# Norm weights as a row spread by TensorE, the first token tile in two column halves, the second tile's squares behind the first's transposes

## The chip, the cores and the metric

The kernel runs on one core of a Trainium2 chip. A core has a matrix engine (TensorE, PE in the profile), a vector engine (VectorE, DVE), a scalar engine (ScalarE, ACT), a general engine (GpSimd, POOL) and a queue engine (SyncE, SP). They run five separate instruction streams, each in its own order, and wait for one another through semaphores. Loads and stores are issued by SP, by POOL or by ACT and are carried out by 16 DMA engines. The metric is the device time of one execution in microseconds, the median of several runs.

## The reference, cut to what matters

```python
def rmsnorm(x, g):
    y = xf * lax.rsqrt(jnp.mean(xf * xf, axis=-1, keepdims=True) + EPS)
    return (y * g).astype(x.dtype)

def reference(x, mem, g_mix_norm, ..., w_in, ...):          # x (1, 1024, 1024), mem (1, 256, 1024)
    h = rmsnorm(x, g_mix_norm[l])
    proj = jnp.einsum('bsd,de->bse', h, w_in[l])            # w_in (1024, 6664)
    ... stick-breaking attention, forgetting attention, memory attention, gates, w_out
    h2 = rmsnorm(x, g_mlp_norm[l])
    u = jax.nn.relu(jnp.einsum('bsd,df->bsf', h2, w_ff_up[l]))
    x = x + jnp.einsum('bsf,fd->bsd', u * u, w_ff_down[l])
```

Only the first line of the block, the norm of x with its weight `g_mix_norm` (1024 numbers, the same for every token), and the first product after it are touched.

## The kernel before, in words

Every product is made from operands split in two parts, a high one (`hi`, `whi`: rounded by an ACT copy) and a low one (`lo`, `wlo`: what is left, by a DVE subtraction), with three matmuls for one: high x high, low x high, high x low. PE therefore has work for nearly the whole time.

The head is the stretch before the first product. The 1024 tokens come in eight tiles of 128 (x0 to x7), each 128 x 1024 floats, 512 KB. For each tile ACT squares it and sums the rows (`norm`, L421) and takes a root (L347); DVE makes the reciprocal root (`rsqrt_quick`, L352 to L361) and scales the tile by it and by the norm weight, in two column halves (L433); PE turns each half by four transposes (`norm_half`, L449); ACT copies the turned half to `hi` (L457) and DVE makes `lo` (L458). The norm weight lies in `gb`, a 128 x 1024 tile, filled by one DMA that repeats the row for all 128 partitions (`fetch_tokens`, L386). The first weight blocks of `w_in`, called w0 and w1 here (rows 0 to 511 and 512 to 1023 of the same 256 columns), are split by `weight` and `split` (L1038, L1039). The first products (L1128, `natural_ops`) are x0 with w0, x0 with w1, x1 with w0 and so on, 12 matmuls each.

While PE has nothing to do at the head, `warm` (L399) gives it dummy transposes of the identity into a bank that nobody reads, two at a time. They have an effect on PE alone.

What sets the order: nothing here is ordered by hand. Each step is a generator that yields operations with an estimated cost, and a planner (`Machine`) runs them against a model clock when the program is built: whenever an engine of the model is free it takes the ready operation with the smallest due time, and the instruction is written into that engine's stream at that moment. `side=True` work (the products, the dummies) is taken only when nothing else is ready. On the chip each engine then runs its stream strictly in order. A dummy that the planner put in front of a product is therefore run before it, whether the product could already start or not. Two more orders matter: SP's own stream (`fetch_tokens`: x0, norm weight, x1, w0, w1, x2 to x7), and a stretch later (at about 47 to 58 us) where the last tokens, two tiles of `mem` and the sums of `sums_T` (L515 to L525) share DVE with the split of two weight blocks of 264 columns.

Of the kernel before, what the change touches and what calls it, by code (L numbers as in the profile page):

```python
# [21 lines left out]
P = 128  # L22
# [21 lines left out]
def tile_hybrid_block(  # L44
# [67 lines left out]
    root_table()  # L112
# [223 lines left out]
    SN, RS, S1 = tiles(E, "sn", 10, 512), tiles(R, "raw", 4, 1024), R.t("s1", [P, 4, 256])  # L336
    XT = tiles(N, "xt", 7, D)
# [8 lines left out]
    def root(z, ss):  # L346
        nc.scalar.activation(z, ss, AF.Sqrt, bias=eps, scale=CUBE ** -2)  # L347
# [24 lines left out]
    def landed(fn, size, *evs):  # L372

        yield from transfer(fn, size, 0.45, 380e3)
        for ev in evs:
            machine.fire(ev)

    def fetch_tokens(keys):
        for key in keys:
            if key[0] == "w":  # L380
                load, (raw, ev) = h_tasks[0].loads[key[1]], first_raws[key[1]]
                spawn(landed(lambda load=load, raw=raw: fetch(raw, load), P * 1024 * 4, ev))
            elif key[0] == "g":
                gb, ev = gains[key[1]]
                g = g_mix if key[1] == "x" else g_memn
                spawn(landed(lambda gb=gb, g=g: nc.sync.dma_start(gb, g.partition_broadcast(P)), P * D * 4, ev))  # L386
            else:
                xt = yield Get(XT)
                src, i = (x, key[1]) if key[0] == "x" else (mem, key[1])
                x_in[key] = xt, spawn(landed(lambda xt=xt, src=src, i=i: nc.sync.dma_start(  # L390
                    xt, src[i * P:(i + 1) * P, :]), P * D * 4))

# [11 lines left out]
    def norm(keys, late, after=None):  # L404
# [6 lines left out]
        for i, key in enumerate(keys):  # L411
            while key not in x_in:
                yield Sleep(0.1)
            xt, ev = x_in[key]
            yield ev
# [9 lines left out]
        r = yield from rsqrt_quick(ss, z, n)  # L425
        for i, key in enumerate(keys):
# [3 lines left out]
            for k4 in range(2):  # L430
# [4 lines left out]
                evs.append(spawn(norm_half(key, xt, k4, last), late))  # L435
            for ev in evs:
# [4 lines left out]
    def norm_half(key, xt, k4, scaled):  # L441
# [15 lines left out]
        yield Op("ACT", act_time(512), lambda: nc.scalar.activation(hi, tr4, AF.Copy))  # L457
        yield Op("DVE", dve_time(512), lambda: nc.vector.tensor_tensor(lo, tr4, f32(hi), ALU.subtract))  # L458
# [21 lines left out]
    def prologue():  # L480
# [3 lines left out]
        spawn(fetch_tokens([("x", 0), ("g", "x"), ("x", 1), ("w", 0), ("w", 1), *xs, ("g", "m"), ("m", 0), ("m", 1)]))  # L484
        spawn(warm(half_made[2, 1]), 100.0)
        evs = [spawn(norm(ks_, 4.0 * i - 8.0, half_made[AFTER[i]] if i in AFTER else None), 4.0 * i - 8.0)
# [549 lines left out]
    def split(hi, lo, raw):  # L1036
        m = int(np.prod(hi.shape[1:]))
        yield Op("ACT", 0.03 + act_time(m), lambda: nc.scalar.activation(hi, raw, AF.Copy))  # L1038
        yield Op("DVE", dve_time(m), lambda: nc.vector.tensor_tensor(lo, raw, f32(hi), ALU.subtract))  # L1039
# [8 lines left out]
    def weight(pair, load, raw):  # L1048
        _, kk, n = load
        if raw is None:  # L1050
# [5 lines left out]
        else:  # L1056
            raw, ev = raw
            yield ev
        yield from split(pair[0][:, :kk * n], pair[1][:, :kk * n], raw[:, :kk * n])
# [1619 lines left out]
```

## Time and profile before

| | |
|---|---|
| median of 3 runs | 1687.49 us (1686.82 to 1692.76) |
| the profiled execution's own time | 1687.17 us |
| its span, first to last instruction | 1685.3 us |
| PE busy | 1673.1 us (99%) |
| DVE busy | 1291.1 us (77%) |
| ACT busy | 848.4 us (50%) |
| first product starts (L1128) | 11.63 us after the span's start |

The profile's times count from the span's start; 1.9 us of the run's time lie outside the span. Rows of the order in time show the start, the duration, the engine, the line, the operation and the tiles that it writes and reads; in brackets stands the idle time ahead and what ended it. PEld rows are weight loads of PE, which run beside its matmuls; SPq rows are the issue of a DMA, not its transfer. A row's duration ends when the last result is written, so that rows which follow closely overlap, and the pace of a stream is read from the starts.

### The profile page before, as it was taken

The page shows a single profiled execution, that of the slowest core. Times are in us where ns is not written, and L with a number is a line of the kernel's source. Part 1 is how long each engine was busy: PE and PEld are TensorE (multiplying, and loading weights), DVE is VectorE, ACT ScalarE, POOL GpSimd, SP SyncE. Part 2 cuts the span into 40 slices and gives each one's busy share as a digit, 9 for nine tenths or more (in the row PEclk, how much of TensorE's full clock was granted, in tenths as well). Part 3 has the DMA queues.
Part 4 walks back from the last instruction along what each step waited for, and adds up shares of the span by engine and source line. Part 5 has one row for each costly group of instructions (what it writes and reads, how often), then busy time and mean ns, then how long its engine had stood idle before and what let it go on. Part 6 is the DMA issues. An engine that isn't in the chain of part 4 may idle for free.

```text
span 1685.3 us, 25009 instructions
## 1 busy us (share of the span) xinstructions
PE 1673.1 (99%) x9118; PEld 1430.1 (85%) x9118; DVE 1291.1 (77%) x2079; ACT 848.4 (50%) x1474; POOL 256.1 (15%) x441
## 2 busy tenths in 40 slices
PE   9999999999999999999999999999999999999999
PEld 9998899998888888888888887778888887888887
DVE  7977778855459888877787898987777776688775
ACT  6455555534358888876762446533333344332331
POOL 0000000000253151254400011022111120000000
PEclk9999999999999999999999999999999999999999
DMA  7545444567384365387757542144444484564532
GB/s 245 158 150 182 148 120 151 146 195 242 128 240 150 113 185 155 116 252 227 222 163 237 181 156 101 57 167 154 148 151 137 150 309 171 199 208 141 196 125 75
DMA packets 141837, 284.32 MB, mean 169 GB/s; under 512 B 16913, under 2 KB 52817, under 8 KB 141714
## 3 DMA queue, kind: packets, MB, share of 16 engines
q1 hardware_dynamic: 110034, 182.56, 32.0%
q0 software_dynamic: 31680, 100.17, 19.8%
q8 instruction: 72, 1.18, 0.3%
q14 instruction: 51, 0.42, 0.1%
HBM read 189.83 MB, written 92.83 MB: 168 GB/s over the span
## 4 chain that ended last, share of the span: by engine, by line
PE 77%; issue 14%; POOL 3%; DVE 3%; DMA 2%; ACT 1%; SPq 0%; POOLq 0%; ACTq 0%; DVEq 0%
PE pp L1416 11%; PE pp L1128 10%; PE sc L1416 7%; PE pp L2616 7%; PE sc L1128 6%; PE tr L901 4%; PE tr L2616 4%; PE sc L2616 4%; POOL s_scr L1956 3%; PE pv L1416 3%; PE pv L2616 2%; PE sc L918 2%; PE pp L918 2%; PE pp L1939 1%; PE pp L2181 1%
## 5 line engine op out<-in xcount | busy, mean ns | idle before, releaser
L1039 DVE TENSOR_TENSOR wlo<-raw,whi 128x1024 fp32r<-128x1024 f32 (+1 forms) x88 | 107.5, 1221 | 80.6 <-ACT whi L1038 80.4
L1038 ACT ACTIVATE whi<-raw 128x1024 fp32r<-128x1024 f32 (+1 forms) x88 | 93.4, 1061 | 80.3 <-PE pp L1416 32.7
L2616 PE MATMUL pp<-h,sop 128*128 128x512 f32 x540 | 128.5, 396 | 0.0
L2616 PEld LDWEIGHTS pp<-h,sop 128*128 128x128 f32 x540 | 101.4, 188 | 24.6 <-DVE sop L1875 0.2
L1939 PE MATMUL pp<-h,oh 128*128 128x512 f32 x384 | 121.1, 396 | 0.7 <-ACT cu L2024 0.6
L908 DVE TENSOR_TENSOR ptl<-tr,pth 128x512 fp32r<-128x512 f32 (+1 forms) x160 | 98.4, 627 | 23.8 <-ACT pth L906 23.4
L906 ACT ACTIVATE pth<-tr 128x512 fp32r<-128x512 f32 (+1 forms) x160 | 86.8, 558 | 32.3 <-PE sc L918 16.8
L1939 PEld LDWEIGHTS pp<-h,oh 128*128 128x128 f32 x384 | 71.9, 188 | 19.0 <-ACT cu L2024 1.4
L2531 ACT ACTIVATE h<-t 128x2048 fp32r<-128x2048 f32 (+1 forms) x17 | 30.8, 1814 | 110.4 <-DVE t L1875 97.6
L1333 POOL DMA_DIRECT2D raw<-w_in x32 | 24.2, 755 | 394.8 <-DVE wlo L1039 394.8
L1939 PE MATMUL pp<-h,ol 128*128 128x512 f32 x192 | 76.0, 396 | 0.0
L827 DVE TENSOR_TENSOR_SCAN e<-r,e 128x384 f32<-128x384 f32 (+3 forms) x64 | 66.3, 1043 | 6.9 <-ACT e L812 6.4
L1932 ACT ACTIVATE oh<-raw 128x512 fp32r<-128x512 f32 x64 | 39.4, 625 | 61.7 <-DVE raw L1875 61.7
L2616 PE MATMUL sc<-h,sop 128*128 128x512 f32 x264 | 63.6, 396 | 0.2 <-DVE sop L1875 0.2
L1875 DVE TENSOR_TENSOR sop<-ur,sop 128x2048 fp32r<-128x2048 f32 (+1 forms) x28 | 61.7, 2208 | 2.2 <-ACT sop L2544 2.2
L2616 PE MATMUL tr<-h,sop 128*128 128x512 f32 x264 | 63.4, 396 | 0.0
L901 PE MATMUL tr<-ident,e 128*128 128x128 f32 x416 | 62.5, 272 | 0.0
L2616 PEld LDWEIGHTS sc<-h,sop 128*128 128x128 f32 x264 | 49.6, 188 | 12.5 <-DVE sop L1875 0.7
L2616 PEld LDWEIGHTS tr<-h,sop 128*128 128x128 f32 x264 | 49.6, 188 | 12.0
L901 PEld LDWEIGHTS tr<-ident,e 128*128 128x128 f32 x416 | 50.7, 140 | 10.3
L1956 POOL DMA_DIRECT2D s_scr<-cu x48 | 26.0, 542 | 197.6 <-DVE cu L1946 189.1
L1933 DVE TENSOR_TENSOR ol<-raw,oh 128x512 fp32r<-128x512 f32 x64 | 43.1, 688 | 16.8 <-ACT oh L1932 16.8
(568 smaller groups left out, 5338.6 us busy)
## 6 DMA issues: line engine op xcount, KB each, us to landing
ur<-s_scr SPq DMA_DIRECT2D x26, 1024.0 KB
raw<-w_in POOLq DMA_DIRECT2D x42, 512.0 KB, 5.1
raw<-w_up SPq DMA_DIRECT2D x60, 256.0 KB
s_scr<-s POOLq DMA_DIRECT2D x60, 256.0 KB, 2.7
g<-w_down SPq DMA_DIRECT2D x14, 1024.0 KB
s_scr<-cu POOLq DMA_DIRECT2D x48, 256.0 KB, 3.0
h<-sbk_scr POOLq DMA_DIRECT2D x64, 128.0 KB, 3.2
o<-gate_scr SPq DMA_DIRECT2D x32, 256.0 KB
```

The lines of the kernel that those rows point to most:

```text
L827: nc.vector.tensor_tensor_scan(out=back, data0=rho[:, :u][:, ::-1], data1=back, initial=0.0 if last else beta[:, c + u:c + u + 1], op0=ALU ...
L901: nc.tensor.transpose(tr[:, jj * 256 + a * P:jj * 256 + (a + 1) * P], es[a][:, j * P:(j + 1) * P], ident)
L906: yield Op("ACT", act_time(512 - lo_c), lambda: nc.scalar.activation(ph[:, lo_c:], tr[:, lo_c:], AF.Copy))
L908: yield Op("DVE", dve_time(512 - lo_c), lambda: nc.vector.tensor_tensor(pl[:, lo_c:], tr[:, lo_c:], f32(ph[:, lo_c:]), ALU.subtract))
L918: nc.tensor.matmul(pv[0][:, c_:256], pair.v[:, j, b, :], p_[:, jj * 256 + c_:(jj + 1) * 256], start=(k == 0 and n_ == 0 and i == 0), stop= ...
L1038: yield Op("ACT", 0.03 + act_time(m), lambda: nc.scalar.activation(hi, raw, AF.Copy))
L1039: yield Op("DVE", dve_time(m), lambda: nc.vector.tensor_tensor(lo, raw, f32(hi), ALU.subtract))
L1128: nc.tensor.matmul(ps, a_, b_, start=(first and i == 0), stop=(last and i == n - 1))
L1416: nc.tensor.matmul(out_, a_, b_, start=(first and n == 0 and j == 0), stop=(last and n == 3 and j == len(todo) - 1), skip_group_check=True)
L1939: nc.tensor.matmul(ps, w[a_][:, k * P:(k + 1) * P], h[b_][k], start=(first and k == 0 and i == 0), stop=(last and k == 3 and i == 2), skip ...
L1956: nc.gpsimd.dma_start(s_scr[r0:r0 + P, :], t)
L2616: nc.tensor.matmul(ps, a_[:, c, qs], b_[:, c, :], start=(kind in ("P1", "P2", "P7") and c == 0 and i == 0), stop=(kind in ("P2", "P4", "P3 ...
```

## The change

- `g_mix` is no longer loaded 128 times over. ACT issues two DMAs of 512 numbers each, first thing in its stream and ahead of the load of its table, into one partition of two `sn` tiles. PE multiplies a row of ones with each of them (`spread_gain`, one matmul each of 128 columns by 512, in float32), which puts the row into all 128 partitions of a PSUM bank. DVE copies the first bank to `gb`, ACT the second.
- x0 is loaded as two DMAs of 512 columns. Its squares are summed in two steps (`first_squares`): the first half's sum becomes the bias of the root and the start of `v`.
- SP's order becomes x0 (two DMAs), w0, x1, w1, x2 and so on.
- x1's squares wait, in the planner, for the second turned half of x0 (`first_turned`); w0's low part waits for x0's scaling (`first_scaled`), w1's split for `first_turned`.
- The planner's rate for transfers is 240e3 instead of 380e3 bytes per us until three tokens' tiles are under way.

```diff
     def root_table():
         nc.scalar.activation(C.t("st", [P, 8])[:, :1], one, AF.Sqrt)
-    root_table()
...
+    gain_rows, ones = [SN.free.popleft() for _ in range(2)], SN.free.popleft()
+    for c, t in enumerate(gain_rows):
+        nc.scalar.dma_start(t[0:1, :], g_mix[:, c * 512:(c + 1) * 512])
+    root_table()
+    nc.vector.memset(ones[0:1, :P], 1.0)
...
-    def rsqrt_quick(ss, z, n):
+    def rsqrt_quick(ss, z, n, v0=-EPS):
...
-        yield Op("DVE", SMALL, lambda: nc.vector.tensor_scalar(v, ss, -1.0, -EPS, ALU.mult, ALU.add))
+        yield Op("DVE", SMALL, lambda: nc.vector.tensor_scalar(v, ss, -1.0, v0, ALU.mult, ALU.add))
...
-        yield from transfer(fn, size, 0.45, 380e3)
+        yield from transfer(fn, size, 0.45, 380e3 if len(x_in) > 2 else 240e3)
...
+                if key == ("x", 0):
+                    evs = [spawn(landed(lambda xt=xt, c=c: nc.sync.dma_start(
+                        xt[:, c * 512:(c + 1) * 512], x[:P, c * 512:(c + 1) * 512]), P * 512 * 4)) for c in range(2)]
+                    first_half.append(evs[0])
+                    x_in[key] = xt, evs[1]
+                    continue
...
+    def spread_gain():
+
+        gb, ev = gains["x"]
+        yield Sleep(2.0)
+        two = yield Get(PP, 2)
+        evs = []
+        for ps, t in zip(two, gain_rows):
+            evs.append((yield Op("PE", 1.7, lambda: nc.tensor.matmul(
+                ps, ones[0:1, :P], t[0:1, :], start=True, stop=True), goes_on=True)))
+        a_, b_ = two
+        yield evs[0]
+        last = yield Op("DVE", dve_time(512), lambda: nc.vector.tensor_copy(gb[:, :512], a_), goes_on=True)
+        yield evs[1]
+        yield Op("ACT", act_time(512), lambda: nc.scalar.activation(gb[:, 512:], b_, AF.Copy))
...
+    def first_squares(xt, ss, z, bias, v0):
+
+        yield first_half[0]
+        yield Op("ACT", 0.85, lambda: nc.scalar.activation(
+            junk[:, :512], xt[:, :512], AF.Square, scale=D ** -0.5, accum_out=v0))
+        yield Op("DVE", 2 * SMALL, lambda: (
+            nc.vector.tensor_scalar(bias, v0, CUBE ** -2, EPS * CUBE ** -2, ALU.mult, ALU.add),
+            nc.vector.tensor_scalar(v0, v0, -1.0, -EPS, ALU.mult, ALU.add)))
+        yield x_in["x", 0][1]
+
+        def rest():
+            nc.scalar.activation(junk[:, 512:], xt[:, 512:], AF.Square, scale=D ** -0.5, accum_out=ss)
+            root(z, ss, bias)
+        yield Op("ACT", 1.1, rest)
...
-        spawn(fetch_tokens([("x", 0), ("g", "x"), ("x", 1), ("w", 0), ("w", 1), *xs, ("g", "m"), ("m", 0), ("m", 1)]))
+        spawn(fetch_tokens([("x", 0), ("w", 0), ("x", 1), ("w", 1), *xs, ("g", "m"), ("m", 0), ("m", 1)]))
...
+        spawn(spread_gain(), -10.0)
+        evs = [spawn(norm(ks_, 4.0 * i - 8.0, first_turned if i == 1 else half_made[AFTER[i]] if i in AFTER else None),
+                     4.0 * i - 8.0)
...
+            if n_ == 1:
+                yield first_turned
+            elif n_ == 0:
+                after = first_scaled
```

What the planner makes of it is seen in the streams. PE's stream before, from its first instruction through the first products; `ident` is the identity, `pv` the bank of the dummies, `tr` the banks of the transposes, xt_150 is x0 and xt_151 is x1, whi_157 and wlo_158 are w0, whi_159 is w1:

```order
L399 MATMUL pv_134<-ident 128x128 x26
L449 MATMUL tr_132<-ident,xt_150 128x128 x4
L449 MATMUL tr_133<-ident,xt_150 128x128 x4
L399 MATMUL pv_134<-ident 128x128 x26
L1128 MATMUL pp_127<-whi_157,hi_120 128x256
...
L399 MATMUL pv_134<-ident 128x128 x2
L1128 MATMUL pp_127<-whi_159,hi_120 128x256
...
L449 MATMUL tr_133<-ident,xt_151 128x128 x4
L399 MATMUL pv_134<-ident 128x128 x10
```

The same place after the change (L445 are the dummies, L501 the transposes, L1192 the products; sn_133, sn_134 the norm weight's rows, sn_135 the ones, xt_153 x0, xt_154 x1, xt_155 x2, whi_160 w0, whi_162 w1):

```order
L445 MATMUL pv_132<-ident 128x128 x2
L412 MATMUL pp_126<-sn_133,sn_135 128x512
L412 MATMUL pp_127<-sn_134,sn_135 128x512
L445 MATMUL pv_132<-ident 128x128 x18
L501 MATMUL tr_130<-ident,xt_153 128x128 x4
L501 MATMUL tr_131<-ident,xt_153 128x128 x4
L445 MATMUL pv_132<-ident 128x128 x14
L1192 MATMUL pp_125<-whi_160,hi_118 128x256
...
L445 MATMUL pv_132<-ident 128x128 x18
L1192 MATMUL pp_125<-whi_162,hi_118 128x256
...
L501 MATMUL tr_131<-ident,xt_154 128x128 x4
L445 MATMUL pv_132<-ident 128x128 x18
L501 MATMUL tr_130<-ident,xt_155 128x128 x4
```

The two spreading products came in after two dummies; up to the first product with w1 and x1 the dummies went from 64 (26, 26, 2, 10) to 70 (2, 18, 14, 18, 18), and those behind the first product from 12 to 36.

ACT's stream before, from its start (xj is a scratch tile, the squares' sums go to `st`):

```order
L111 ACT_TABLE_LOAD
L111 ACTIVATE st_72<-sm 128x1
L421 ACTIVATE xj_167,st_170<-xt_150 128x1024
L347 ACTIVATE st_171<-st_170,sm 128x1
L421 ACTIVATE xj_167,st_172<-xt_151 128x1024
L347 ACTIVATE st_173<-st_172,sm 128x1
L1038 ACTIVATE whi_157<-raw_163 128x1024
L457 ACTIVATE hi_120<-tr_132 128x4x128
```

And after:

```order
L338 DMA sn_133<-g_mix 1x512
L338 DMA sn_134<-g_mix 1x512
L111 ACT_TABLE_LOAD
L111 ACTIVATE st_150<-sm 128x1
L427 ACTIVATE xj_170,st_189<-xt_153 128x512
L435 ACTIVATE xj_170,st_173<-xt_153 128x512
L351 ACTIVATE st_174<-st_173,st_189 128x1
L418 ACTIVATE gb_168<-pp_127 128x512
L1094 ACTIVATE whi_160<-raw_166 128x1024
L509 ACTIVATE hi_118<-tr_130 128x4x128
L509 ACTIVATE hi_118<-tr_131 128x4x128
L471 ACTIVATE xj_170,st_175<-xt_154 128x1024
```

The squares of x1 moved from ahead of w0's high part to behind x0's turned halves, and the copy of the spread weight stands between x0's root and w0.

DVE's stream before, where the last tokens' low part (L458) meets the sums (L515 to L525) and the two blocks of 264 columns (wlo of 1056):

```order
L458 TENSOR_TENSOR lo_121<-tr_133,hi_120 128x4x128
L515 TENSOR_TENSOR sn_143<-hi_120 128x512
...
L525 TENSOR_TENSOR sn_135<-sn_135,lo_121 128x512
L1039 TENSOR_TENSOR h_752<-sn_144,h_751 128x512
L1039 TENSOR_TENSOR h_750<-sn_143,h_749 128x512
L1039 TENSOR_TENSOR wlo_162<-raw_164,whi_161 128x1056
L1039 TENSOR_TENSOR h_754<-sn_135,h_753 128x512
L1039 TENSOR_TENSOR wlo_158<-raw_163,whi_157 128x1056
```

And after:

```order
L512 TENSOR_TENSOR mt_123<-tr_130,mt_122 128x512
L512 TENSOR_TENSOR mt_123<-tr_131,mt_122 128x512
L571 TENSOR_TENSOR sn_134<-hi_118 128x512
...
L581 TENSOR_TENSOR sn_136<-sn_136,lo_119 128x512
L1097 TENSOR_TENSOR h_779<-sn_135,h_778 128x512
L1097 TENSOR_TENSOR wlo_165<-raw_167,whi_164 128x1056
L1097 TENSOR_TENSOR wlo_161<-raw_166,whi_160 128x1056
```

The last tile ahead of the sums is now one of `mem` (mt) and no longer of x, and one split of a sum instead of two stands ahead of the first wlo, none between the two. Behind about 110 us of the program the streams of all five engines are the same as before.

More of the change, by code (lines that the diff above doesn't have):

```diff
@@ L414, in norm @@
             xt, ev = x_in[key]
+            if key == ("x", 0):
+                two = stat(2)
+                yield from first_squares(xt, ss, z, two[:, 0:1], two[:, 1:2])
+                continue
             yield ev
@@ L424, in norm @@
             yield Op("ACT", 1.25 + 0.22 * last, squares)
-        r = yield from rsqrt_quick(ss, z, n)
+        r = yield from rsqrt_quick(ss, z, n, two[:, 1:2] if keys[0] == ("x", 0) else -EPS)
         for i, key in enumerate(keys):
@@ L1034, in __init__, with split @@
             self.done, self.chosen, self.w = Event(), Event(), []
-    def split(hi, lo, raw):
+    def split(hi, lo, raw, after=None):
         m = int(np.prod(hi.shape[1:]))
         yield Op("ACT", 0.03 + act_time(m), lambda: nc.scalar.activation(hi, raw, AF.Copy))
+        if after:
+            yield after
         yield Op("DVE", dve_time(m), lambda: nc.vector.tensor_tensor(lo, raw, f32(hi), ALU.subtract))
@@ L1049, in weight @@
         _, kk, n = load
+        after = None
         if raw is None:
@@ L1056, in weight @@
         else:
+            n_ = next((i for i, r_ in enumerate(first_raws) if r_ is raw), None)
             raw, ev = raw
             yield ev
-        yield from split(pair[0][:, :kk * n], pair[1][:, :kk * n], raw[:, :kk * n])
+            if n_ == 1:
+                yield first_turned
+            elif n_ == 0:
+                after = first_scaled
+        yield from split(pair[0][:, :kk * n], pair[1][:, :kk * n], raw[:, :kk * n], after)
         RAW.put(raw)
```

14 lines of the change are left out of this document (11 added, 3 removed).

## The prediction

> **What bounds the kernel now.** I read the page's busy table first, then PE's waits over the whole span, then PE's time by stretches, then the head row by row.
>
> ```profile
> PE 1673.1 (99%) x9118; PEld 1430.1 (85%) x9118; DVE 1291.1 (77%) x2079; ACT 848.4 (50%) x1474; POOL 256.1 (15%) x441
> ```
>
> PE is busy but for 12.2 us of 1685.3. Its waits, with what ended them (us in total, times, longest):
>
> ```profile
> PE tr L449 <- DVE xt L433: 1.4, 1, 1.4
> PE pv L399 <- POOL ident masks.py:199: 1.4, 1, 1.4
> PE pp L1128 <- DVE wlo L1039: 1.1, 2, 0.9
> PE pp L1128 <- DVE lo L458: 0.2, 1, 0.2
> ```
>
> Those at the head are 1.4 (x0's scaling), 0.2 and, near 57 us, 1.1. PE's time by stretches (us from the start, length, busy, count):
>
> ```profile
> 6.31:7.72 1.41, 0.01 (x2) 1.00 1.00 373
> 7.72:11.60 3.88, 3.87 (x33) 1.00 1.08 388
> 11.60:19.62 8.02, 7.84 (x67) 1.00 1.05 381
> 19.62:49.96 30.34, 30.34 (x266) 1.00 0.44 145
> ```
>
> From 19.62, the first product of w1 with x1, PE has no gap for 30 us. So whatever the change does to the moment at which PE reaches that product shifts all behind it by as much, until the wait near 57 us. The busy share hides one thing: dummies count as busy. Before the first product the chain that ended last runs through a transfer and not through PE (start, length, what):
>
> ```profile
> 2.12 7.17 DMA raw<-w_in
> ...
> 9.32 1.07 ACT whi L1038
> ...
> 10.41 1.01 DVE wlo L1039
> ...
> 11.55 0.69 DVE lo L458
> ...
> 12.29 1.44 PE pp L1128 x10
> 13.73 0.22 PE pv L399 x2
> ```
>
> w0 lands at 9.3 and its split and x0's low part end at 12.25. The change aims at this chain.
>
> **The change, part by part.** The rows needed, PE's first, then ACT, DVE and SP:
>
> ```profile
> 1.36 4.95 PE L399 MATMUL pv<-ident 128*128 128x128 f32 x26 [1.36 <-POOL ident masks.py:199]
> 7.72 1.32 PE L449 MATMUL tr<-ident,xt 128*128 128x128 f32 x8 [1.40 <-DVE xt L433]
> 8.87 3.00 PE L399 MATMUL pv<-ident 128*128 128x128 f32 x26
> 11.63 0.36 PE L1128 MATMUL pp<-whi,hi 128*128 128x256 f32 x1
> 12.29 0.38 PE L1128 MATMUL pp<-whi,lo 128*128 128x256 f32 x1 [0.18 <-DVE lo L458]
> 12.51 0.28 PE L1128 MATMUL pp<-whi,hi 128*128 128x256 f32 x1
> 13.45 0.28 PE L1128 MATMUL pp<-whi,lo 128*128 128x256 f32 x1
> 19.62 0.36 PE L1128 MATMUL pp<-whi,hi 128*128 128x256 f32 x1
> ```
>
> ```profile
> 0.74 1.28 ACT L111 ACT_TABLE_LOAD   x1 [0.74 <-PEq L2668]
> 4.75 1.06 ACT L421 ACTIVATE xj<-xt 128x1024 f32<-128x1024 f32 x1 [2.52 <-DMA xt<-x]
> 5.71 0.19 ACT L421 ACTIVATION_READ_ACCUMULATOR xj<-xt 128x1 f32 x1
> 5.94 0.30 ACT L347 ACTIVATE st<-st,sm 128x1 f32<-128x1 f32 x1
> 7.82 1.06 ACT L421 ACTIVATE xj<-xt 128x1024 f32<-128x1024 f32 x1 [1.58 <-DMA xt<-x]
> 10.28 1.07 ACT L457 ACTIVATE hi<-tr 128x512 fp32r<-128x512 f32 x2
> ```
>
> ```profile
> 6.91 1.41 DVE L433 SCALAR_TENSOR_TENSOR xt<-xt,st,gb 128x512 f32<-128x512 f32 x2
> 10.41 1.23 DVE L1039 TENSOR_TENSOR wlo<-raw,whi 128x1024 fp32r<-128x1024 f32 x1 [0.47 <-ACT whi L1038]
> 11.55 1.28 DVE L458 TENSOR_TENSOR lo<-tr,hi 128x512 fp32r<-128x512 f32 x2
> ```
>
> ```profile
> 0.74 0.39 SPq L390 DMA_DIRECT2D xt<-x  x1
> 1.18 0.42 SPq L386 DMA_DIRECT2D gb<-g_mix  x1
> ```
>
> *Paces.* 26 dummies fill PE's stream from 8.77 (the weight load of the first) to 11.60, 0.109 each; products go at (13.45 - 12.51)/8 = 0.1175. The early dummies take longer, as two windows of PE's dummies show:
>
> ```profile
> 1.30:3.30 2.00, 1.94 (x9) 1.94 (x10) 1.00 0.68 221
> 5.30:6.30 1.00, 1.00 (x9) 0.78 (x7) 1.00 0.99 381
> ```
>
> 9 in 2.0 us, later 9 in 1.0: 0.22 against 0.11. 25 steps from 1.36 to the last start at 5.93 give 17 at 0.22 and 8 at 0.11, so PE went to full speed near 5.2, 3.9 us after its first dummy.
>
> *Transfers.* The broadcast of the norm weight (512 KB) leaves the queue. x0 is there at 4.75 and x1, with that broadcast between, at 7.82: about 1.5 us for 512 KB. So w0 lands at 4.75 + 1.6 = 6.4 instead of 9.3, x1 at 7.9 (unchanged), w1 at 9.4, x2 and all behind it 1.5 us earlier. The extra issue of x0's second half costs SP 0.4 us, hidden behind the transfers that already run.
>
> *Norm weight.* ACT's two DMA issues (0.39 each, as SP's) put its table load from 0.74 to 1.6 and the end of it to 3.1, hidden: ACT is idle until 4.75. When the rows land no row shows. The DMA's rate in slices of 0.3 us gives the bounds:
>
> ```profile
> GB/s 0 0 0 0 0 27 205 150 410 369 314 382 273 232 259 218 314 232 369 423 396 423 335 379 375 389 376 389 358 362 358 379 355 423 437 396 410 396 382 396
> ```
>
> The first bytes move in 1.5 to 1.8, the lower end is 1.8; the upper is 4.75, if the rows arrive with x0. x0's 512 KB have moved by 3.5 and ACT sees them at 4.75, 1.25 later; 1.8 and some 1.0 of such a lag give 2.8, which I take. Then the two float32 products of 512 columns. No row has a float32 product that is no transpose: four dummies at 0.22 hold 512 columns and take 0.9, the lower end; twice that, 1.8, is my upper end for full precision, and I take 1.7, near the upper end, since all other products here run in the split format. They end at T0 = 2.8 + 3.4 = 6.2. DVE's copy (about 0.65, as half of L458's 1.28) is done by 5.2, ACT's (half of L457's, 0.55) by 6.9.
>
> *x0.* Its second half lands with the whole tile's bytes, 4.75. Half the squares are left: 0.55 instead of 1.06, so L433 starts at 6.4 instead of 6.91 and the first transpose may go at 7.2 instead of 7.72. x1's squares, put behind x0's turned halves, cost nothing: PE needs x1 only at about 16.
>
> *PE's stream.* This decides. From T0 to the first product of w1 with x1 stand 18 + 14 + 18 + 18 = 68 dummies, 24 transposes and 36 products. Transposes cost about a dummy: 92 x 0.109 + 36 x 0.1175 = 14.26. The same counting for before, from 12.29 (34 products, 12 dummies, 16 transposes), gives 7.05 where the trace has 7.33, so I add 0.3 for changes between kinds: T0 + 14.56. With T0 = 6.2 that is 20.76; 3 of the first dummies fall before full speed (6.7, that is 3.9 after 2.8), 0.3 more: 21.1. Before it was 19.62. **+1.45.** Nothing else is as late: transposes of x0 at 6.2 + 0.3 + 18 x 0.109 = 8.5 (its scaled half is there at 7.2), first product at 8.5 + 22 x 0.109 = 10.9, a good 0.7 earlier than 11.63, with w0's split done at 9.2 and x0's first low part at about 10.4; on ACT x0's turned halves are copied by 10.1, x1's squares and root done by 11.6 (1.55), w1's high part by 12.7 (1.06), its low part on DVE by 13.9 (1.23), where PE wants it at 10.9 + 1.4 + 18 x 0.109 = 14.3. So the chain through w0 is shortened as meant, and PE then gives the time back on 24 more dummies behind the first product (24 x 0.109 = 2.6).
>
> *Near 57 us.* DVE's rows there:
>
> ```profile
> 49.17 0.68 DVE L515 TENSOR_TENSOR sn<-hi 128x512 f32<-128x512 f32 x1
> 55.31 1.26 DVE L1039 TENSOR_TENSOR wlo<-raw,whi 128x1056 fp32r<-128x1056 f32 x1
> 57.09 1.25 DVE L1039 TENSOR_TENSOR wlo<-raw,whi 128x1056 fp32r<-128x1056 f32 x1
> ```
>
> The 1.1 us are 0.9 for the first wlo and 0.2 for the second. With one split less ahead (0.6), but the last tile turned later (one of `mem`), I leave the 0.9 as it is, between 0 and 1.8; the second wlo now follows the first directly, and its 0.2 goes. Behind that place the streams are the same.
>
> *Sum.* +1.45 - 0.2 = +1.25 on the profiled execution's 1687.17: **1688.4**. The median before, 1687.49, is 0.3 above that execution.
>
> **A rule that would raise it.** The trace has one step of PE to full speed, 3.9 us after the first dummy. The Trainium skill, in TensorE: Matmul & The Clock Gate, Part 1, says that the array runs at half speed until a free-running window of about 3.4 us has been busy, and that the moment varies with where the window falls; 3.9 agrees. By that rule the gap that PE now has between its second dummy and the first row's landing may cost a window: full speed then comes between 6.2 and 9.6.
>
> **The rivals.** *PE's full speed comes late.* If a product with one row of 128, or the gap ahead of it, doesn't count, the 3.9 us start with the dummies at 6.2. All 18 then take 0.22, 18 x 0.109 = 2.0 more instead of 0.3: +1.45 + 1.7 - 0.2 = +2.9, 1690.1. Against it speaks that the early dummies needed no full load either; for it, that no row shows a one-row product. *Not slower:* the float32 products are cheap (0.9 each, T0 = 4.6), and PE waits for x0 again. Its transposes, the 50 dummies behind them and the rest are 74 x 0.109 + 36 x 0.1175 + 0.3 = 12.6, so PE arrives earlier than 19.62 if x0's first transpose starts before 7.0, that is if the second half lands before 4.5. Landing at 4.2 gives 6.7 and -0.3; with the 0.2 that is 1686.7. For it speaks the rate row: x0's bytes have moved by 3.5. Against it, the 4.75 at which ACT saw the same bytes. *The weight comes no sooner than the tokens* (the change doesn't do what it says): rows at 4.75, T0 = 8.15 at full speed in the second half, 22.7, +3.1 - 0.2, 1690.1.
>
> **How the numbers follow.** Forecast (PE runs its stream from the spread on, +0.3 to +2.4 by the bounds of the landing and of the product) 0.60, 1688.4. Late full speed 0.20, cheap spread 0.12, late rows 0.08. The range takes in the first two rivals' times and 0.4 for the runs' spread around their median, and a wait near 57 us half gone below: 1686.3 to 1691.0. All cases lie within 0.5% (8.4 us, about what a measurement of this kernel can tell from no change): 0.97; 0.01 faster; 0.02 slower, for a place downstream that I haven't seen.
>
> **What would show it.** In the profile of the changed kernel: w0's high part should start before 8 us (right: the transfer moved up); the first product before 11.3; PE without a wait from the spread to 21 us, with 18 dummies between the products of w0 and of w1; the first product of w1 with x1 near 21.1; the two L412 matmuls about 1.7 apart. A gap of PE ahead of x0's transposes would show the cheap spread; dummies at 0.22 behind the spread, the late full speed. Wrong I am if PE waits behind the first product, so that the dummies cost nothing, or if the stall near 57 us changes by more than 0.5.

## The result, and the profile after

The changed kernel takes 1692.40 us (median of 12 runs, 1691.02 to 1696.03); the kernel before, run beside it, 1688.98 (median of 12, 1686.51 to 1692.76). The ratio is 1.002, with a 95% interval of 1.0012 to 1.0028: slower by 2.0 to 4.7 us. That is clear of noise, and still within the bound of 0.5% under which the prediction counts two times as the same. The profiled execution took 1695.19 us with a span of 1693.4, 8.1 more than the span before.

PE in order of time from the first instruction (start, duration, what, idle time ahead in brackets); L445 are the dummies, L412 the spreading products, L501 the transposes, L1192 the products:

```profile
1.36 0.69 PE L445 MATMUL pv<-ident 128*128 128x128 f32 x2 [1.36 <-POOL ident masks.py:199]
2.40 3.75 PE L412 MATMUL pp<-sn,sn 1*128 1x512 f32 x4 [0.35 <-DMA sn<-g_mix]
6.08 4.10 PE L445 MATMUL pv<-ident 128*128 128x128 f32 x18
9.97 1.64 PE L501 MATMUL tr<-ident,xt 128*128 128x128 f32 x8
11.44 1.69 PE L445 MATMUL pv<-ident 128*128 128x128 f32 x14
12.89 0.36 PE L1192 MATMUL pp<-whi,hi 128*128 128x256 f32 x1
...
14.39 2.12 PE L445 MATMUL pv<-ident 128*128 128x128 f32 x18
...
18.64 2.13 PE L445 MATMUL pv<-ident 128*128 128x128 f32 x18
...
22.89 0.28 PE L1192 MATMUL pp<-whi,hi 128*128 128x256 f32 x1
```

The last row is the first product of w1 with x1: 22.89 where it was 19.62, 3.27 later. Three groups of 18 dummies stand in this piece. The later two take 2.12 and 2.13 us, the first 4.10: it ran at half speed to its end. PE's time by stretches says the same by its counts (from, to, length, busy and instructions):

```profile
6.08:11.19 5.11, 5.11 (x25) 5.11 (x25) 2.70 (x4) 1.78 (x3) 0.00 (x0) 1.00 1.03 395
11.19:22.89 11.70, 11.70 (x106) 11.70 (x105) 9.12 (x23) 8.74 (x17) 0.00 (x0) 1.00 0.99 359
```

25 instructions in 5.11 us, 0.204 each, then 106 in 11.70, 0.110 each. The trace's record of the granted clock begins with full speed at 11.19 us (before: at 5.29). The column of the granted clock reads 1.00 in both rows, since the record has nothing ahead of its first entry: at the head the pace of the starts is the evidence.

ACT and DVE at the same place:

```profile
6.18 0.60 ACT L418 ACTIVATE gb<-pp 128x512 f32<-128x512 f32 x1 [0.69 <-PE pp L412]
7.70 1.06 ACT L1094 ACTIVATE whi<-raw 128x1024 fp32r<-128x1024 f32 x1 [0.92 <-DMA raw<-w_in]
11.07 1.18 ACT L509 ACTIVATE hi<-tr 128x512 fp32r<-128x512 f32 x2 [2.31 <-PE tr L501]
```

```profile
6.18 1.41 DVE L483 SCALAR_TENSOR_TENSOR xt<-xt,st,gb 128x512 f32<-128x512 f32 x2
8.79 1.23 DVE L1097 TENSOR_TENSOR wlo<-raw,whi 128x1024 fp32r<-128x1024 f32 x1 [1.20 <-ACT whi L1094]
11.70 1.29 DVE L512 TENSOR_TENSOR lo<-tr,hi 128x512 fp32r<-128x512 f32 x2 [1.68 <-ACT hi L509]
```

The transfer of w0 did move up (its high part starts at 7.70, before at 9.32), and x0 is scaled from 6.18 (before 6.91). Now ACT waits 2.31 us for PE's transposes, and DVE 1.68 for ACT: the roles at the head are turned round.

PE's waits over the whole span, of the changed kernel:

```profile
PE pv L909 <- DVE st L914: 3.9, 1, 3.9
PE pp L2327 <- ACT h L2302: 2.1, 1, 2.1
PE pv L445 <- POOL ident masks.py:199: 1.4, 1, 1.4
PE pp L1192 <- DVE wlo L1097: 1.1, 2, 0.8
```

The 1.4 for x0 is gone, the 1.1 near 57 us are what they were. One wait far behind the change has grown: 3.9 us near 745 us, where the kernel before had 1.5. Behind it the granted clock was 0.51 for 7 us (first the row of PE before and after the change, then two stretches after it):

```profile
743.80 0.50 PE L853 MATMUL pv<-h,h 128*128 128x512 f32 x1 [1.46 <-DVE st L858]
```

```profile
749.16 0.80 PE L909 MATMUL pv<-h,h 128*128 128x512 f32 x1 [3.94 <-DVE st L914]
```

```profile
744.00:748.40 4.40, 1.22 (x6) 0.66 (x4) 2.01 (x4) 2.46 (x4) 0.78 (x1) 1.00 0.98 309
748.40:755.40 7.00, 6.24 (x20) 5.15 (x20) 4.36 (x15) 3.84 (x9) 0.00 (x0) 0.51 0.54 188
```

So the profiled execution lost about 3.3 us at the head and about 5 near 745. The second loss is found in the kernel before too: one of its three profiled executions waits 3.85 us there and loses two windows of the clock (table below). A mean granted clock of 0.998 or less, which two such windows give, stands in 3 of the changed kernel's 12 runs and in 17 of the 68 runs of the kernel before that were taken beside the experiments. That is the same share, and nothing here puts this loss down to the change.

### The profile page after: what moved, and what is told of

Same layout as the page of the kernel before. It is cut to its first block, busy times and chain, and to the rows that moved or that the text cites. A ratio compares the mean times of both kernels' runs of the same rounds, so it can differ in the third digit from the quotient of the medians.

```text
span 1693.4 us, 25041 instructions
## 1 busy us (share of the span) xinstructions
PE 1679.9 (99%) x9128; PEld 1434.4 (85%) x9128; DVE 1293.1 (76%) x2083; ACT 849.6 (50%) x1477; POOL 256.9 (15%) x441
## 4 chain that ended last, share of the span: by engine, by line
PE 94%; DVE 3%; DMA 1%; ACT 1%; issue 0%; ACTq 0%; DVEq 0%
PE pp L1480 11%; PE pp L1192 10%; PE pp L2003 10%; PE pp L2680 8%; PE sc L1480 7%; PE sc L1192 6%; PE sc L2003 5%; PE sc L2680 4%; PE tr L2680 4%; PE tr L957 4%; PE pv L1480 3%; PE pv L2680 3%; PE tr L2003 2%; PE sc L974 2%; PE pp L974 2%; PE pp L2245 1%
```

## The experiments

Some places to compare by: the moment of full speed in the clock record, the first product, the second product of the split near 57 us (the one that waits for `wlo`, 56.62 before and 59.87 after), and PE's arrival at the stop near 745 us (the start of its row there less the wait ahead of it). "Later half speed" counts windows of 3.41 us at half speed in the rest of the profiled execution, without the piece at its very end that every execution has. Ratios are to the kernel before in the same job, where its medians were 1689.38 (beside one_row, all_rows, no_spread and late_spread_no_dummies) and 1690.36 (beside fewer_dummies, the two rows_97 kernels and before_w0_first).

| kernel | full speed | first product | near 57 | arrives at the stop | wait there | later half speed | median, ratio (95%) |
|---|---|---|---|---|---|---|---|
| before | 5.29 | 11.63 | 56.62 | 742.34 | 1.46 | 0 | 1688.98 beside the changed one |
| changed | 11.19 | 12.89 | 59.87 | 745.22 | 3.94 | 2 | 1692.40, 1.002 (1.0012 to 1.0028) |
| one_row | 13.64 | 15.54 | 62.52 | 747.86 | 2.44 | 1 | 1694.73, 1.003 (1.002 to 1.004) |
| all_rows | 7.29 | 11.66 | 58.63 | 743.95 | 1.46 | 0 | 1690.35, 1.0005 (0.9995 to 1.0016) |
| no_spread | 4.62 | 13.03 | other order | 743.55 | 1.55 | 0 | 1689.59, 0.9996 (0.9987 to 1.0005) |
| late_spread_no_dummies | 17.00 | 11.42 | 58.25 | 743.94 | 2.05 | 1 | 1690.94, 1.0007 (0.9997 to 1.0016) |
| fewer_dummies | 10.37 | 12.62 | 58.60 | 745.01 | 3.39 | 2 | 1693.76, 1.0014 (1.0004 to 1.0023) |
| rows_97 | 7.28 | 10.81 | 57.79 | 743.13 | 1.61 | 0 | 1689.99, 1.0006 (0.9995 to 1.0016) |
| rows_97_few_dummies | 7.32 | 9.52 | 55.89 | 741.55 | 2.97 | 1 | 1690.29, 1.0004 (0.9995 to 1.0014) |
| before_w0_first | 6.41 | 11.72 | 57.59 | 744.59 | 2.89 | 4 | 1691.58, 1.0013 (1.0004 to 1.0023) |
| changed, again (a, b) | 10.97, 9.51 | 12.66, 11.95 | 59.63, 58.92 | 744.95, 744.21 | 2.13, 1.46 | 1, 1 | one run each: 1691.96, 1690.51 |
| before, again (a, b) | 5.05, 6.55 | 11.47, 11.49 | 56.65, 57.02 | 742.34, 742.73 | 3.85, 2.18 | 4, 0 | one run each: 1695.36, 1687.92 |

**Does a product that feeds one row count towards full speed?** The theory was that it doesn't; the rival, that the gap ahead of the products is to blame. Two kernels with the same edit but for one thing: both zero the two row tiles first, so that all 128 partitions may be read, and the transfers of the rows wait for that.

`one_row`, the product as in the changed kernel:

```diff
     for c, t in enumerate(gain_rows):
+        nc.vector.memset(t, 0.0)
         nc.scalar.dma_start(t[0:1, :], g_mix[:, c * 512:(c + 1) * 512])
...
-    nc.vector.memset(ones[0:1, :P], 1.0)
+    nc.vector.memset(ones[:, :P], 1.0)
```

> The changed kernel with one delay added: DVE clears the two tiles that take the norm weight's rows before the DMAs may fill them, so the rows land about 0.7 us later; the products still use one row. It is the control for the run with all rows. Theory A (a product that feeds one row of the array does not count towards PE's full speed) and theory B (the gap behind the second dummy, or the phase of a window, decides, whatever is fed) both expect PE at half speed through all 18 dummies behind the spread, full speed near 11 us, the first product of w0 at 13 to 14 us, and 3.5 to 4.5 us over the kernel before.

`all_rows`, the same and the product over all rows (127 of them zero):

```diff
-                ps, ones[0:1, :P], t[0:1, :], start=True, stop=True), goes_on=True)))
+                ps, ones[:, :P], t, start=True, stop=True), goes_on=True)))
```

> As the run with one row, with the same delay and the same instructions, but each spreading product feeds all 128 rows of the array (ones in every row against the weight in the first and zeros in the others); the result is the same. Theory A expects full speed between 5 and 8 us, the dummies behind the spread at 0.11 each, the first product at 10.5 to 11.5 us and the time about 2.5 us under the run with one row. Theory B expects no difference between the two: full speed near 11 us, first product at 13 to 14 us.

The products and the 18 dummies behind them, one_row first, then all_rows:

```profile
4.09 2.04 PE L413 MATMUL pp<-sn,sn 1*128 1x512 f32 x2 [2.04 <-DMA sn<-g_mix]
6.91 2.07 PE L413 MATMUL pp<-sn,sn 1*128 1x512 f32 x2 [0.78 <-DMA sn<-g_mix]
8.90 4.10 PE L446 MATMUL pv<-ident 128*128 128x128 f32 x18
```

```profile
3.91 3.63 PE L413 MATMUL pp<-sn,sn 128*128 128x512 f32 x4 [1.85 <-DMA sn<-g_mix]
7.38 2.13 PE L446 MATMUL pv<-ident 128*128 128x128 f32 x18
```

all_rows has a gap of 1.85 us ahead of its products, five times the changed kernel's 0.35, and yet its 18 dummies take 2.13 us. Their times are told apart as well: the intervals of the two ratios, 1.002 to 1.004 and 0.9995 to 1.0016, don't meet. The expectation for one_row missed its sizes: the delay was to be about 0.7 us, but its products start 1.7 and, the second, 2.7 us later than in the changed kernel, and full speed (13.64) and the first product (15.54) came later than it said; all_rows' first product, 11.66, just missed its 10.5 to 11.5 too. In one_row PE also waits 0.78 us for the second row, in all_rows not, so the two differ in one more thing than meant. `rows_97` mends that: the row lies in partition 96, rows 0 to 95 are zeroed beside its transfer, and the transfer waits for nothing.

```diff
-        nc.scalar.dma_start(t[0:1, :], g_mix[:, c * 512:(c + 1) * 512])
+        nc.scalar.dma_start(t[96:97, :], g_mix[:, c * 512:(c + 1) * 512])
...
+    for t in gain_rows:
+        nc.vector.memset(t[0:96, :], 0.0)
...
-                ps, ones[0:1, :P], t[0:1, :], start=True, stop=True), goes_on=True)))
+                ps, ones[0:97, :P], t[0:97, :], start=True, stop=True), goes_on=True)))
```

> The gain row lies in partition 96, rows 0 to 95 are zeroed, and the product feeds 97 rows instead of one; the row's transfer does not wait for the zeroing. Theory 'a one-row product does not count towards full speed': full speed between 5.8 and 9.2 us instead of 11.2, the two products still end near 6.1, the first product of w0 at 10.5 to 11.5 (12.9), the first product of w1 with x1 at 20.6 to 21.7 (22.9), the time about 2 us under the changed kernel's and 1 to 2 over the kernel before. Rival 'the gap ahead of the products closes the count, whatever they feed': full speed at 10 to 12 and the time of the changed kernel.

```profile
2.22 3.78 PE L414 MATMUL pp<-sn,sn 97*128 97x512 f32 x4 [0.17 <-DVE sn L342]
5.79 2.86 PE L447 MATMUL pv<-ident 128*128 128x128 f32 x18
8.49 1.04 PE L503 MATMUL tr<-ident,xt 128*128 128x128 f32 x8
9.36 1.69 PE L447 MATMUL pv<-ident 128*128 128x128 f32 x14
10.81 0.36 PE L1194 MATMUL pp<-whi,hi 128*128 128x256 f32 x1
...
20.82 0.28 PE L1194 MATMUL pp<-whi,hi 128*128 128x256 f32 x1
```

The two products take as long with 97 rows (3.78 us) as with one (3.75), the dummies behind them start 0.3 us earlier, and full speed comes at 7.28 instead of 11.19. The first product of w1 with x1 comes at 20.82, 2.07 earlier than in the changed kernel, and near 57 us the kernel stands 1.17 behind the one before. The theory holds, and the gap does not explain it. How many rows it takes between 1 and 97 was not tried. In time rows_97 is not told apart from the kernel before (ratio 1.0006); the interval of the changed kernel's 1.002 meets its own at the edge, so that these two times alone would not show the gain.

**When exactly does full speed come?** In each clock record all changes are whole multiples of 3.413 us apart (changed kernel: 748.47 - 11.19 = 737.28 = 216 x 3.4133; 755.30 - 748.47 = 6.83), but where the first one falls differs from run to run. Two more executions of each kernel, unchanged:

> The changed kernel once more, unchanged: is the moment of full speed drawn anew in each execution? Theory 'the clock is judged in back-to-back windows of 3.41 us whose phase differs from run to run, and a window with one-row products in it doesn't count': the two products end at 6.1, so full speed comes at the end of the first window that begins after that, anywhere from 9.5 to 12.9 us. Rival 'it comes a fixed time after the first whole matmul': 11.2 again within 0.3.

> As the run after_again_a: by the windows full speed anywhere from 9.5 to 12.9 us, by the rival 11.2 within 0.3; the stop near 745 us of one, two or no half-speed windows, whichever the moment of the last transfer gives.

> The kernel before once more, unchanged. Theory 'windows of free phase': its first dummies run from 1.4 to 6.3 us (later where they go at half speed to the end), so full speed comes between 4.8 and 6.9 where a whole window falls among them, and else not before x0's transposes have been followed by a busy window, after 11 us; then the head costs about what the changed kernel's does. Rival 'a fixed time after the first dummy': 5.3 again within 0.3.

> As the run before_again_a: by the windows full speed between 4.8 and 6.9 us or after 11, by the rival 5.3 within 0.3; the stop near 745 us of one, two or no half-speed windows.

The 18 dummies of the changed kernel in its two (a, then b):

```profile
5.83 4.10 PE L445 MATMUL pv<-ident 128*128 128x128 f32 x18
```

```profile
5.83 3.96 PE L445 MATMUL pv<-ident 128*128 128x128 f32 x18
```

Full speed came at 10.97 and 9.51, both between 9.5 and 12.9; before at 5.05 and 6.55, both between 4.8 and 6.9. In all fourteen profiled executions one rule gives the moment: it is the end of the first window of 3.413 us in which PE is busy throughout (but for up to 0.2 us at its start) with transposes or products that feed many rows. In the changed kernel's first profile the window from 4.36 to 7.78 was busy throughout but held one-row products until 6.08, and the clock stayed at half until the next had passed; in rows_97 the window from 3.87 to 7.28 was the same but for the rows, and counted. The fixed delay (11.2 again, 5.3 again, within 0.3) has fallen by the executions b. The rule that the Trainium skill gives in TensorE: Matmul & The Clock Gate, Part 1, free-running windows of about 3.4 us, agrees with these multiples; that some products don't count in them is what the runs add.

The kernel before doesn't feel the phase at its head: with full speed at 5.29, 5.05 and 6.55 its first product of w1 with x1 came at 19.62, 19.64 and 19.66, because x0 and w0 come later than its dummies end. Near 57 us it stood at 56.62, 56.65 and 57.02; 0.36 of the last came in only between 33 and 35 us. The changed kernel passes the phase on: 22.89, 22.66 and 21.95 at that product, and 59.87, 59.63 and 58.92 near 57 us. Even the best of them is 1.9 behind the last of the others.

**What is the rest of the change worth?** `no_spread` keeps the column halves and the squares' place and takes the spread out; the norm weight comes by its repeating DMA, behind x0's halves.

```diff
-    gain_rows, ones = [SN.free.popleft() for _ in range(2)], SN.free.popleft()
-    for c, t in enumerate(gain_rows):
-        nc.scalar.dma_start(t[0:1, :], g_mix[:, c * 512:(c + 1) * 512])
...
-        spawn(fetch_tokens([("x", 0), ("w", 0), ("x", 1), ("w", 1), *xs, ("g", "m"), ("m", 0), ("m", 1)]))
+        spawn(fetch_tokens([("x", 0), ("g", "x"), ("w", 0), ("x", 1), ("w", 1), *xs, ("g", "m"), ("m", 0), ("m", 1)]))
...
-        spawn(spread_gain(), -10.0)
```

> The change without the spread: the norm weight is loaded 128 times over as before, behind x0's two halves and ahead of w0; x0 in halves, x1's squares behind x0's turn and the order w0, x1, w1 stay. Theory A and B: dummies from 1.36 us without a break, full speed near 5.3 us as before, x0's transposes near 7.2, first product near 11 us. Behind it stand 20 dummies (12 before the change): the first product of w1 with x1 near 19.4 to 19.9, so within 0.5 us of the kernel before. If instead the halves or the new order cost something by themselves, it is more than 1 us slower.

```profile
1.36 5.50 PE L441 MATMUL pv<-ident 128*128 128x128 f32 x34 [1.36 <-POOL ident masks.py:199]
9.12 1.32 PE L497 MATMUL tr<-ident,xt 128*128 128x128 f32 x8 [2.26 <-DVE xt L479]
10.28 3.00 PE L441 MATMUL pv<-ident 128*128 128x128 f32 x26
13.03 0.36 PE L1187 MATMUL pp<-whi,hi 128*128 128x256 f32 x1
```

```profile
8.31 1.41 DVE L479 SCALAR_TENSOR_TENSOR xt<-xt,st,gb 128x512 f32<-128x512 f32 x2 [2.33 <-DMA gb<-g_mix]
```

A miss: x0's scaling now waits for the weight until 8.31, its transposes with it, w0's split starts at 9.74 and the first product comes at 13.03, later than in either kernel; the first product of w1 with x1 comes at 20.77 and not by 19.9. The stop near 745 is reached 1.2 later than before, yet the time is that of before within its interval. Without the spread the halves have nothing to gain from: the weight lands last.

`before_w0_first` takes the order of the transfers alone into the kernel before, w0 ahead of x1, with its dummies ended at x0's turn.

```diff
-        spawn(fetch_tokens([("x", 0), ("g", "x"), ("x", 1), ("w", 0), ("w", 1), *xs, ("g", "m"), ("m", 0), ("m", 1)]))
-        spawn(warm(half_made[2, 1]), 100.0)
+        spawn(fetch_tokens([("x", 0), ("g", "x"), ("w", 0), ("x", 1), ("w", 1), *xs, ("g", "m"), ("m", 0), ("m", 1)]))
+        spawn(warm(half_made[0, 1]), 100.0)
```

> The kernel before with one transfer moved, w0 ahead of x1, and the dummies ended at x0's turn; no spread, no column halves. Theory 'what the change gains is the place of w0 in the queue, and the spread only costs': w0 lands near 7.9 us instead of 9.3, the first product comes at 10.3 to 10.7 instead of 11.6, the first product of w1 with x1 at 18.5 to 19.5 instead of 19.6, the time 0 to 1 us under the kernel before. Rival 'the next transfer takes the place of w0': TensorE waits for x1 or w1 instead, the first product of w1 with x1 stays within 0.3 us of 19.6 and the time is that of before.

```profile
8.02 1.06 ACT L1038 ACTIVATE whi<-raw 128x1024 fp32r<-128x1024 f32 x1 [1.91 <-DMA raw<-w_in]
9.34 1.06 ACT L421 ACTIVATE xj<-xt 128x1024 f32<-128x1024 f32 x1 [0.27 <-DMA xt<-x]
...
10.73 1.06 ACT L457 ACTIVATE hi<-tr 128x512 fp32r<-128x512 f32 x2
```

A miss. w0 lands 1.3 earlier, as expected, but x1's squares (9.34) still stand ahead of x0's copies on ACT (10.73, before 10.28), and the planner put 28 dummies there; the first product came at 11.72, 0.1 later than before, the first product of w1 with x1 at 20.16, which neither the theory nor the rival had, and PE stood 1.0 behind near 57 us. The time is slower than before, by a ratio of 1.0004 to 1.0023. The place of w0 in the queue is worth nothing by itself, with ACT's order as it is: w0 was one of two things that the first product waited for.

`late_spread_no_dummies` puts the 18 dummies ahead of the products and leaves out all the later ones:

```diff
-        yield Sleep(2.0)
+        yield Sleep(5.6)
...
-        while not until.fired:
-            yield Op("PE", 0.43 if machine.now < 7.5 else 0.22, turns, 0.0, side=True)
+        for _ in range(9):
+            yield Op("PE", 0.43, turns, 0.0, side=True)
```

(In addition w0's split waits for the spread weight's copies, and the planner counts a spreading product as 0.95 us.)

> The change with 18 dummies ahead of the spread instead of 2, and no dummy behind it: PE is fed whole-array work without a break for 3.9 us first. w0's high part also waits for the copy of the weight. Theory A: full speed near 5.3 us, before or during the two products, which then take about 0.95 each; x0's transposes near 7.7, first product near 10.2 us; PE waits for w1's split (about 13) and for x1, where the changed kernel runs dummies, and the first product of w1 with x1 is at 18 to 19 us, 1 us under the kernel before and some 4 under the changed one. Theory B: the same, as there is no gap. If dummies are needed to hold full speed, the products behind the first are at half speed and it is slower than before.

```profile
1.37 4.10 PE L445 MATMUL pv<-ident 128*128 128x128 f32 x18 [1.37 <-POOL ident masks.py:199]
5.40 3.78 PE L412 MATMUL pp<-sn,sn 1*128 1x512 f32 x4
9.11 1.12 PE L501 MATMUL tr<-ident,xt 128*128 128x128 f32 x4
```

Another miss, for both theories: the first product of w1 with x1 came at 21.39 and not at 18 to 19. Its 18 dummies fill 4.03 us and don't bring full speed: no whole window lay inside them (its edges fall at 3.34 and 6.76), one-row products followed, then short waits, and full speed came at 17.00. That it still stands at 58.25 near 57 us, ahead of the changed kernel with a full speed six microseconds later, suggests that the 50 dummies behind x0's turn cost something there; how much, the next kernel shows.

**Does PE give the time back on its dummies?** `fewer_dummies` ends them in the changed kernel at x0's turn, 34 fewer behind the first product.

```diff
-        spawn(warm(half_made[2, 1]), 100.0)
+        spawn(warm(half_made[0, 1]), 100.0)
```

> The changed kernel with its dummies ended at x0's turn instead of x1's: 34 fewer behind the first product (2, 18, 14 and then 2). Theory 'TensorE gives the time back on the dummies': it reaches the first product as the changed kernel does (12.9 us where full speed comes at 11, earlier where it comes earlier), x1's transpose and the first product of w1 with x1 then come earlier by up to 34 x 0.109 = 3.7 us, less what the transfers or the split of w1 make it wait: 21 to 22 instead of 22.9, the time 0.5 to 2 us under the changed kernel's. Rival 'the dummies cost nothing, another chain sets the moment': the first product of w1 with x1 stays within 0.3 us of 22.9, with TensorE waiting where the dummies stood, and the time is the changed kernel's.

The first product of w1 with x1 came at 21.78, as the theory said. 34 x 0.109 = 3.7 us left out moved PE by 1.27 near 57 us (58.60), of which 0.27 stood at the first product already, from an earlier full speed. Most of the rest turned into waits for splits: in its trace PE waits 0.88 for `wlo`, 0.25 for `hi` and 0.77 for `lo` between 15 and 20 us. So the dummies did cost, but only about 1.0 us is to be had from them. By the stop near 745 it had lost most of that too (745.01, 0.2 ahead): 0.51 of it in a wait for `wlo` at 107.26 us that the changed kernel doesn't have. Its time is not told apart from the changed kernel's.

`rows_97_few_dummies` is the attempt to beat both kernels: rows_97, 8 dummies behind the spread, 12 behind x0's turn, none later.

```diff
-        while not until.fired:
-            yield Op("PE", 0.43 if machine.now < 7.5 else 0.22, turns, 0.0, side=True)
+        for n_ in range(5):
+            yield Op("PE", 0.43, turns, 0.0, side=True)
+        yield first_moved
+        for n_ in range(6):
+            yield Op("PE", 0.22, turns, 0.0, side=True)
```

> As rows_97, with dummies only where TensorE would else wait: 8 behind the spread, 12 behind x0's turn, none behind the first product. If dummies are what the head pays with, the first product of w0 comes at 10 to 10.7 us, the first product of w1 with x1 at 18.8 to 19.5, and the time is 0 to 1 us under the kernel before. Rival 'without them full speed comes late, as in the run with the spread moved behind the dummies': full speed after 13 us, the first product of w1 with x1 after 20, and the time 1 us or more over the kernel before.

```profile
9.52 0.36 PE L1199 MATMUL pp<-whi,hi 128*128 128x256 f32 x1
...
11.50 0.38 PE L1199 MATMUL pp<-whi,hi 128*128 128x256 f32 x1 [0.33 <-ACT whi L1101]
12.76 0.39 PE L1199 MATMUL pp<-wlo,hi 128*128 128x256 f32 x1 [0.88 <-DVE wlo L1104]
```

The head comes out ahead, as the theory said: first product at 9.52 (11.63 before, and sooner than the 10 to 10.7 expected), the first product of w1 with x1 at 18.88 (19.62), and 55.89 near 57 us, 0.73 ahead of the kernel before. PE then waits for w1's split, as the rows show. In the time this doesn't appear: ratio 1.0004, interval 0.9995 to 1.0014, which neither shows a gain nor excludes one of 0.8 us.

## Why the prediction was wrong

It said 1688.4 with a range of 1686.3 to 1691.0; it was 1692.4. The chance for no change by 0.5% was right.

*The step that failed* is "3 of the first dummies fall before full speed (6.7, that is 3.9 after 2.8)": it let the spreading products count towards full speed. One-row products don't (rows_97, all_rows), and full speed came at 11.19. From 6.08 to 11.19 PE got half of the work done that it does at full speed: 5.11 / 2 = 2.55 us lost in place of 0.3. Of the head's +3.27 where +1.45 was forecast, this is the whole excess and more (2.25; T0 was 0.12 early and another 0.3 was not needed). This was the first rival, with a chance of 0.20. Its size was short too: it let only the 18 dummies go at half speed; x0's transposes did as well, since a whole window had to begin behind the products.

*The sum of PE's stream* stands once that is put right. With T0 the start of the 18 dummies, F the moment of full speed, and the 14.26 of the prediction, the first product of w1 with x1 should come at T0 + 14.26 + (F - T0) / 2 (the last term where F is behind T0):

| run | T0 | F | sum | measured |
|---|---|---|---|---|
| changed | 6.08 | 11.19 | 22.90 | 22.89 |
| changed, again a | 5.83 | 10.97 | 22.66 | 22.66 |
| changed, again b | 5.83 | 9.51 | 21.93 | 21.95 |
| one_row | 8.90 | 13.64 | 25.53 | 25.54 |
| all_rows | 7.38 | 7.29 | 21.64 | 21.66 |
| rows_97 | 5.79 | 7.28 | 20.80 | 20.82 |

The 0.3 "for changes between kinds" was not needed. rows_97, whose full speed came close to where the prediction put it, shows what the prediction described: +1.20 at that product and +1.17 near 57 us, for a forecast of +1.45 and +1.25.

*The terms.* T0 was 6.08 for 6.2, from two misses that cancel by luck: the row landed for PE at 2.40, not 2.8 (at 2.16 or earlier in the two later executions), and a product took 1.84, not 1.7. w0's high part at 7.70 met "before 8 us", though the sum had w0 land at 6.4, 1.3 too early; PE did not wait for it. PE ran without a wait from the spread to 22 us, as said. The first product at 12.89 missed "before 11.3" by the failed step alone: in rows_97 it came at 10.81. The 0.2 near 57 us didn't go (1.1 in two waits, as before). That PE gives the time back on dummies was right as to where it went, but of the 3.7 us of dummies that fewer_dummies leaves out only about 1.0 came back.

*The base.* 1.25 was added to one execution of 1687.17, near the median of the three runs shown. Beside the changed kernel the median of before was 1688.98, and later 1689.38 and 1690.36. So of the miss of 4.0 us, 3.4 - 1.25 = 2.2 is the difference between the kernels and 1688.98 - 1687.17 = 1.8 the base: 0.4 for the runs' spread was far too little. Either one alone would have left the time inside the range (1687.17 + 3.4 = 1690.6; 1688.98 + 1.25 = 1690.2). That the range reaches 1691.0 was not worked out either: the rivals' 1690.1 and the 0.4 give 1690.5, and at the lower end 1686.7 - 0.4 = 1686.3 leaves nothing for a wait near 57 us half gone.

The execution that served as base was one with a mean granted clock of 1.000. Of the kernel before, 11 of 68 runs have that, and their median is 1687.8; the 17 with 0.998 or less have 1692.2. The changed kernel's two runs at 1.000 took 1691.0 and 1691.3, so the head's loss of 3.3 us shows there too, as far as two runs can say. The list of waits in the prediction names four; the two longest of the kernel before, 1.6 us near 1023 and 1.5 near 743, are not among them, and the second is the stop near 745 us that the last section takes up.

## What to carry to other kernels

A matmul with a contraction of one row costs as much time as a full one here (3.75 us for two, 3.78 with 97 rows) and does nothing for TensorE's clock; where it stands ahead of the first heavy work, feed it many rows (97 were enough here, and zeros will do) or put it behind a full busy window. Where a head has slack behind transfers, the moment of full speed is hidden; a change that uses up that slack exposes the moment and its phase, so both have to enter the sum. Filler work in an engine's stream is free only as long as something later than it sets the pace.

## What the runs showed of the hardware that was not expected

A transfer far from the change takes part in the spread between runs. Near 745 us ACT waits for the last piece of `o_scr` to come back, DVE for ACT, PE for DVE (of the changed kernel, DMA from the chain that ended last, then ACT; last the same row of the kernel before, executed again, a):

```profile
735.12 10.80 DMA r<-o_scr
```

```profile
745.94 1.67 ACT L1094 ACTIVATE h<-r 128x512 fp32r<-128x512 f32 x3 [2.53 <-DMA r<-o_scr]
```

```profile
742.97 1.67 ACT L1038 ACTIVATE h<-r 128x512 fp32r<-128x512 f32 x3 [2.44 <-DMA r<-o_scr]
```

PE's wait there was 1.46 to 3.94 us in the fourteen profiled executions, in both kernels. It is ACT's wait for the transfer and 1.4 us on top: 2.53 and 3.94, 2.44 and 3.85, 0.73 and 2.13. In three executions (before, all_rows, changed again b) ACT did not wait for the transfer, and PE waited 1.46. The kernel before, executed again, had 3.85 and four windows at half speed (two here and two near 1030 us) and took 1695.36 us, then 2.18, none and 1687.92.

A long wait closes the clock for one or two windows of 3.413 us, each worth up to 1.7 us. It was two in the six cases in which the wait reached into the next window, and one in the other five: as at the head, the clock opens behind a window that is busy throughout. Whether it closes depends again on the phase. A wait of 2.18 us that straddled the edge of two windows (1.10 and 1.08) did not close it. Over the stops near 745 and near 1030 us, ten windows in which PE stood still for 1.9 us or more in one piece all closed it, and none with 1.8 or less did but one, with 1.46 (changed again b); so the bound isn't settled. The Trainium skill, in TensorE: Matmul & The Clock Gate, Part 1, has the clock fall back to half speed after an idle window of about 3.4 us; here 1.46 us without work was once enough.

What delays the transfer isn't settled either, and no run here tried it. Its toll went from nothing to about 5 us (the changed kernel's first profiled execution), which is a likely reason that a shift of under a microsecond at the head can't be read from the medians of some twelve runs, though the traces show it.
